# A two-block network in fp32 on one core: weight splits in pieces of 512 columns, broadcasts by transposes, and a reordered end of the last down projection

## The chip, the cores and the metric

The kernel runs on one core of one Trainium2 chip. The metric is the device time of one execution in microseconds (us); lower is better. Five engines of the core take part: TensorE (PE in the profile; its weight loads are listed apart as PEld), VectorE (DVE), ScalarE (ACT), GpSimd (POOL) and SyncE (SP), which issues the DMA transfers. Each engine works through its own list of instructions in order, and waits on semaphores for the others.

## The reference

256 tokens `x` and 256 context tokens `ctx` of width 1024 go through two networks of two layers each. What matters here, cut short:

```python
def first_block(x, c, ctx, c_ctx, ...):            # layer 0: convolution, layer 1: attention
    for i in range(DEPTH):
        hx = rmsnorm(x, norm_g[i, 0]) * (1.0 + sc_x) + sh_x
        ...                                          # conv_module or attention_module
        x = x + g_x * rmsnorm(yx, norm_g[i, 1])
        fx = rmsnorm(x, norm_g[i, 2]) * (1.0 + scf_x) + shf_x
        x = x + gf_x * rmsnorm(swiglu(fx, ffn_w1[i], ffn_w3[i], ffn_w2[i]), norm_g[i, 3])
    return x

def second_block(x, ...):
    for l in range(DEPTH):
        mix = token_mixing(x, ...)                   # three branches, two of them attention
        x = layer_norm(ALPHA * x + mix, ln1_g[l], ln1_b[l])
        ffn = conv_ffn(x, ...)                       # (gelu(a) * u) @ w_down
        x = layer_norm(ALPHA * x + ffn, ln2_g[l], ln2_b[l])
    return x
```

All matrices are fp32, and the result has to have about fp32 accuracy.

## The kernel before

**Products.** Activations lie transposed, features on the 128 partitions and tokens along the free dimension. A product in fp32 accuracy is made of three products in the reduced type fp32r: both operands are split into a rounded part "hi" and the rest "lo", and `mm3` (or `mm_late`, the same in another order) adds hi·hi, hi·lo and lo·hi in PSUM. The tiles of hi and lo parts are called `round` in the profile (`late` where they share room that an earlier phase gave up); everything else in SBUF is `plain`, and PSUM tiles are `bank`.

**Weights.** All weights lie in one DRAM tensor `wts`, in chunks of 128 x 2048 in the order of use. `Stream.next` issues a chunk's DMA, and `Stream.split` makes hi and lo of each half of it (128 x 1024): ScalarE copies the half to hi (a CAST with rounding), VectorE subtracts hi from the source to get lo. Three chunks may be in flight and five halves of hi and lo may be held.

**Normalisations.** `rms` and `ln_stats` sum over features on TensorE, get one number for each token, `y`, with the tokens on partitions, raise it to the power -0.5 on GpSimd (`rsqrt`), and call `spread`, which turns `y` into a PSUM tile that has the token's number in every partition: for each block of 128 tokens a plain fp32 matmul of the broadcast column `y[:, t:t+1]` with the identity matrix. `rms` spreads 2 blocks; `ln_stats` spreads mean and scale, 4 blocks each at the convolution's end and 2 blocks each elsewhere; `diff_norm` in `mixing` spreads twice 4 blocks in each of its two layers. `normed` in `layer1` does the same with its own code for the keys, twice 4 blocks. Counted over the program these are 62 matmuls of `spread` (26 from `rms`, 20 from `ln_stats`, 16 from `diff_norm`) and 8 of `normed`, 70 in all. `trans` in `layer1` and in `mixing` transposes 128 x 128 blocks of attention weights by TensorE's transpose, with the same identity.

**The last down projection.** `conv_ffn` of the last layer calls `updown` with `tokens`: here the product with `w_down` is made with tokens on the partitions, in four PSUM banks, one for each block of 128 tokens (t = 0, 1) and half of the 1024 outputs (o = 0, 1). `down_tokens(c)` adds the two hidden tiles of chunk c; the last chunk is c = 10. Then `final` normalises and writes block t = 0 and then t = 1: two BN_STATS, BN_AGGR, an addition, the power on GpSimd and a small product, then for each half an activation on ScalarE, a product and an addition on VectorE, and the DMA of 128 x 512 to `out`.

**What sets the order.** Nothing runs when the code above is called: `Recorder` notes every instruction and what it depends on, and `schedule` puts all of them in an order by a list scheduler with costs for each instruction (`cost`: 111 ns for a transpose, about 220 ns for a plain fp32 matmul of 128 columns; for VectorE and ScalarE a constant and a slope), in several rounds, of which it keeps the best. `emit` then issues them in that order from one line (L889 of the profile, so lines tell nothing apart), and `fills` puts idle-time fillers, plain 128 x 128 matmuls of identity by identity into an unused bank, into those gaps of the plan in which TensorE would stand still (L883). So a change of a single operation can move any instruction of the program.

Of the kernel before, what the change touches and what calls it, by code (L numbers as in the profile page):

```python
# [10 lines left out]
F32 = mybir.dt.float32  # L11
# [8 lines left out]
D = 1024  # L20
T = 256
KT = 8
FT = 22
# [16 lines left out]
FOLD1 = 2  # L40
ROUNDS = 6
SWITCH = 95
RUSH = 20e3
FILL = 0.7

# [859 lines left out]
class Stream:  # L905
# [18 lines left out]
    def split(self, src):  # L924
        n = src.shape[1]
        hi, lo = (self.pool.tile([128, HALF], F32R, tag=g, bufs=self.nsp) for g in ("hi", "lo"))
        self.nc.scalar.copy(hi[:, :n], src)
        self.nc.vector.tensor_sub(lo[:, :n], src, hi[:, :n].bitcast(F32))
        return hi, lo


class Kern:
# [145 lines left out]

    def spread(self, out, y):

        n = y.shape[-1]
        for t in range(n):
            self.nc.tensor.matmul(out[:, t * 128:t * 128 + 128], y[:, t:t + 1].to_broadcast([128, 128]), self.cst("ident"),
                                  start=(t == 0), stop=(t == n - 1))

    def feature_means(self, tiles, tag):

# [471 lines left out]
    def layer1(self):  # L1559
        nc, tc, xs = self.nc, self.tc, self.xs  # L1560
        with ExitStack() as es:
# [19 lines left out]
            def normed(src, g, name):  # L1581

                y = head_rms(src)
                b, ye = self.bank("tp", "hr"), self.s512("ye")
                nc.scalar.copy(ye.rearrange("p (a b) -> p a b", a=8), y[:, :, None].to_broadcast([128, 8, 64]))
                for t in range(4):
                    nc.tensor.matmul(b[:, t * 128:t * 128 + 128], ye[:, t * 128:t * 128 + 128], self.cst("ident"),
                                     start=(t == 0), stop=(t == 3))
                q = self.s512(name)
                nc.scalar.mul(q, src, g)  # L1590
                nc.vector.tensor_mul(q, q, b)
                return q
# [150 lines left out]
    def updown(self, up_, label, banks, tokens=None):  # L1743

        hs = {}

        def down_tokens(c):
            w = self.ws.next(label + (c,))
            last = c == FT // 2 - 1
            if last:  # L1750
                order = [(kk, t, o) for t in range(2) for o in range(2) for kk in range(2)]
            else:
                order = [(kk, t, o) for kk in range(2) for t in range(2) for o in range(2)]
            for kk, t, o in order:
                k, cols = 2 * c + kk, slice(t * 128, t * 128 + 128)
                self.mm3(banks[2 * t + o], hs[k][0][:, cols], hs[k][1][:, cols], *w.hl(kk * D + o * 512, 512),
                         k == 0, k == FT - 1)
            if c == 0:
                tokens()

        def down(c):
            if tokens:
                return down_tokens(c)
            w = self.ws.next(label + (c,))
            last = c == FT // 2 - 1
            if last:
                order = [(kk, m) for m in range(8) for kk in range(2)]
            else:
                order = [(kk, m) for kk in range(2) for m in range(8)]
            for kk, m in order:  # L1770
                k, b = 2 * c + kk, kk * 8 + m
                self.mm3(banks[m // 2][:, (m % 2) * T:(m % 2) * T + T], *w.hl(b * 128, 128), hs[k][0], hs[k][1],
                         k == 0 and m % 2 == 0, k == FT - 1 and m % 2 == 1)

        for j in range(FT):
            hs[j] = up_(j)
            if j >= 2 and j % 2 == 0:
                down(j // 2 - 1)
        down(FT // 2 - 1)
# [559 lines left out]
```

## Time and profile before

| what | value |
|---|---|
| time before, median of 3 runs | 1916.68 us (1913.9 to 1918.26) |
| the profiled execution's own time | 1914.48 us |
| its span from the first to the last instruction | 1912.7 us |
| mean granted TensorE clock | 0.997 |
| TensorE busy | 1885.2 us, 99% of the span |
| VectorE busy | 1398.7 us, 73% |
| ScalarE busy | 1094.4 us, 57% |

The profile is of one execution. Its own time is 1.8 us longer than its span, and 2.2 us below the median of the runs. Busy time counts an engine from an instruction's start to its end, waits excluded. A plain fp32 matmul shows as two records in the trace, an fp32r matmul and a transpose as one.

### The profile page before, as it was taken

To read this page: it belongs to the slowest core of one execution; us is meant where nothing else is said; L and a number is where in the kernel's file an instruction comes from. 1 tells how busy PE (TensorE), PEld (TensorE's weight loads), DVE (VectorE), ACT (ScalarE), POOL (GpSimd) and SP (SyncE) were. 2 spreads that over 40 slices of the span, in tenths; PEclk is the share of its full clock that TensorE was granted. 3 is DMA by queue.
4 is the path that set the end of the run, shared out by engine and by line. 5 is a ranking of instruction groups with operands and counts; after the bars stand their busy time and mean duration, and the time that the engine had idled before them with its cause. 6 is when DMAs were issued, how large, how long until landed. Compare 5 with 4: busy or idle time off the path is not lost.

```text
span 1912.7 us, 35502 instructions
## 1 busy us (share of the span) xinstructions
PE 1885.2 (99%) x14444; PEld 1721.3 (90%) x14444; DVE 1398.7 (73%) x2535; ACT 1094.4 (57%) x1913; POOL 321.9 (17%) x297
## 2 busy tenths in 40 slices
PE   8999999999999999999999999999999999999997
PEld 5765988999998878999999999999999999998997
DVE  5996878878877686655479755786679976577666
ACT  5576845444535587544557555575567665556554
POOL 0674000000001311000032001331114200123001
PEclk9999999999999999999999999999999999999999
DMA  8367534323325441455434544444544444454552
GB/s 351 132 231 304 186 125 162 122 98 111 114 93 192 154 155 67 175 179 198 155 135 155 179 155 154 156 177 176 199 139 174 150 182 155 155 166 166 190 185 88
DMA packets 44949, 312.53 MB, mean 163 GB/s; under 512 B 5489, under 2 KB 5745, under 8 KB 8433
## 3 DMA queue, kind: packets, MB, share of 16 engines
q1 hardware_dynamic: 44784, 310.26, 45.0%
q8 instruction: 113, 1.85, 0.4%
q14 instruction: 52, 0.42, 0.1%
HBM read 309.19 MB, written 1.05 MB: 162 GB/s over the span
## 4 chain that ended last, share of the span: by engine, by line
PE 87%; DVE 6%; ACT 4%; DMA 1%; issue 1%; POOL 0%; SPq 0%; DVEq 0%; POOLq 0%; ACTq 0%
PE bank L889 87%; DVE plain L889 3%; DVE round L889 3%; ACT plain L889 2%; ACT round L889 2%; PE bank L883 1%; DMA plain<-vecs 0%; POOL plain L889 0%; DVE late L889 0%; DMA plain<-wts 0%; DMA plain<-xin 0%; ACT L889 0%; ACT early L889 0%; SPq L889 0%; POOLq L2334 0%
## 5 line engine op out<-in xcount | busy, mean ns | idle before, releaser
L889 PE MATMUL bank<-round 128*128 128x256 f32 (+2 forms) x8912 | 1185.9, 291 | 2.9 <-ACT round L889 1.8
L889 PEld LDWEIGHTS bank<-round 128*128 128x128 f32 x8912 | 1120.6, 189 | 53.0 <-issue 17.5
L889 DVE TENSOR_TENSOR round<-plain,round 128x1024 fp32r<-128x1024 f32 (+2 forms) x581 | 659.0, 1153 | 314.5 <-ACT round L889 311.7
L889 ACT CAST round<-plain 128x1024 fp32r<-128x1024 f32 (+4 forms) x573 | 547.1, 974 | 437.2 <-PE bank L889 390.7
L889 PE MATMUL bank<-late,round 128*128 128x256 f32 (+1 forms) x2780 | 408.1, 300 | 1.3 <-DVE late L889 1.0
L889 PEld LDWEIGHTS bank<-late,round 128*128 128x128 f32 x2780 | 373.8, 191 | 24.3 <-issue 4.0
L889 POOL TENSOR_TENSOR plain<-plain 128x256 f32<-128x256 f32 (+6 forms) x181 | 212.2, 1183 | 848.0 <-DVE plain L889 538.1
L889 PE MATMUL bank<-plain 128*128 128x128 f32 (+9 forms) x1894 | 217.4, 373 | 11.2 <-ACT plain L889 9.3
L889 ACT ACTIVATE plain<-plain 128x256 f32<-128x256 f32 (+6 forms) x361 | 152.3, 446 | 106.1 <-DVE plain L889 90.1
L889 PEld LDWEIGHTS bank<-plain 128*32 128x32 f32 (+4 forms) x1894 | 132.5, 141 | 64.8 <-issue 27.1
L889 DVE TENSOR_TENSOR plain<-plain 128x256 f32<-128x256 f32 (+6 forms) x324 | 135.2, 445 | 23.8 <-ACT plain L889 10.5
L889 DVE TENSOR_TENSOR plain<-plain,bank 128x256 f32<-128x256 f32 (+1 forms) x236 | 115.2, 508 | 40.4 <-PE bank L889 32.6
L889 ACT COPY plain<-bank 128x512 f32<-128x512 f32 (+5 forms) x189 | 92.1, 503 | 75.9 <-PE bank L889 70.9
L889 POOL MEMSET late<- 64x1024 f32 (+2 forms) x14 | 8.6, 612 | 649.6 <-PE bank L889 649.2
L889 ACT ACTIVATE plain<-bank,plain 128x256 f32<-128x256 f32 (+3 forms) x171 | 95.9, 602 | 28.4 <-PE bank L889 12.3
L889 ACT CAST late<-plain 128x256 fp32r<-128x256 f32 (+2 forms) x114 | 56.2, 493 | 75.2 <-DVE plain L889 58.7
L889 POOL TENSOR_TENSOR plain<-plain,early 128x512 f32<-128x512 f32 x79 | 89.5, 1135 | 55.5 <-ACT early L889 51.4
L889 DVE SCALAR_TENSOR_TENSOR bank<-early,plain,bank 128x512 f32<-128x512 f32 x130 | 90.4, 749 | 1.0
L889 ACT ACTIVATE round<-plain 128x256 fp32r<-128x256 f32 (+2 forms) x128 | 62.8, 534 | 30.8 <-DVE plain L889 19.6
L889 DVE SCALAR_TENSOR_TENSOR plain<-plain,bank 128x256 f32<-128x256 f32 (+1 forms) x138 | 63.9, 508 | 19.4 <-PE bank L889 18.9
L889 DVE TENSOR_TENSOR late<-plain,late 128x256 fp32r<-128x256 f32 (+2 forms) x106 | 57.2, 540 | 17.4 <-ACT late L889 17.3
L889 PE MATMUL bank<-round,late 128*128 128x512 f32 x264 | 63.3, 393 | 1.4 <-ACT late L889 1.2
(61 smaller groups left out, 785.5 us busy)
## 6 DMA issues: line engine op xcount, KB each, us to landing
plain<-wts SPq DMA_DIRECT2D x280, 1024.0 KB, 4.8
plain<-wts SPq DMA_DIRECT2D x8, 768.0 KB, 4.2
plain<-xin SPq DMA_DIRECT2D x2, 1024.0 KB, 7.3
early<-wts SPq DMA_DIRECT2D x2, 1024.0 KB, 16.7
plain<-wts SPq DMA_DIRECT2D x2, 840.0 KB, 4.4
plain<-lnv SPq DMA_DIRECT2D x2, 512.0 KB, 4.6
out<-plain SPq DMA_DIRECT2D x4, 256.0 KB, 2.0
plain<-consts SPq DMA_DIRECT2D x1, 736.0 KB, 9.7
```

Of the source, the lines that this page charges most:

```text
L883: self.nc.tensor.matmul(self.banks[b][:, :128], *map(real, fill), start=True, stop=True)
L889: getattr(on, name)(*map(real, a), **{n: real(x) for n, x in k.items()})
```

## The change

Three edits, and a constant `PART = 512`:

```diff
@@ class Stream @@
     def split(self, src):
         n = src.shape[1]
         hi, lo = (self.pool.tile([128, HALF], F32R, tag=g, bufs=self.nsp) for g in ("hi", "lo"))
-        self.nc.scalar.copy(hi[:, :n], src)
-        self.nc.vector.tensor_sub(lo[:, :n], src, hi[:, :n].bitcast(F32))
+        for c in range(0, n, PART):
+            s = slice(c, min(c + PART, n))
+            self.nc.scalar.copy(hi[:, s], src[:, s])
+            self.nc.vector.tensor_sub(lo[:, s], src[:, s], hi[:, s].bitcast(F32))
         return hi, lo
@@ class Kern @@
     def spread(self, out, y):
-        n = y.shape[-1]
-        for t in range(n):
-            self.nc.tensor.matmul(out[:, t * 128:t * 128 + 128], y[:, t:t + 1].to_broadcast([128, 128]), self.cst("ident"),
-                                  start=(t == 0), stop=(t == n - 1))
+        for t in range(y.shape[-1]):
+            self.nc.tensor.transpose(out[:, t * 128:t * 128 + 128], y[:, t:t + 1].to_broadcast([128, 128]), self.cst("ident"))
@@ layer1, normed @@
                 for t in range(4):
-                    nc.tensor.matmul(b[:, t * 128:t * 128 + 128], ye[:, t * 128:t * 128 + 128], self.cst("ident"),
-                                     start=(t == 0), stop=(t == 3))
+                    nc.tensor.transpose(b[:, t * 128:t * 128 + 128], ye[:, t * 128:t * 128 + 128], self.cst("ident"))
@@ updown @@
         def down_tokens(c):
-            w = self.ws.next(label + (c,))
-            last = c == FT // 2 - 1
-            if last:
-                order = [(kk, t, o) for t in range(2) for o in range(2) for kk in range(2)]
+            ws[c] = self.ws.next(label + (c,))
+            end = FT // 2 - 2
+            if c < end:
+                order = [(2 * c + kk, t, o) for kk in range(2) for t in range(2) for o in range(2)]
+            elif c == end:
+                order = [(2 * c + kk, 0, o) for kk in range(2) for o in range(2)]
             else:
-                order = [(kk, t, o) for kk in range(2) for t in range(2) for o in range(2)]
-            for kk, t, o in order:
-                k, cols = 2 * c + kk, slice(t * 128, t * 128 + 128)
-                self.mm3(banks[2 * t + o], hs[k][0][:, cols], hs[k][1][:, cols], *w.hl(kk * D + o * 512, 512),
+                order = [(2 * c + kk, 0, o) for o in range(2) for kk in range(2)]
+                order += [(2 * end + kk, 1, o) for o in range(2) for kk in range(4)]
+            for k, t, o in order:
+                cols = slice(t * 128, t * 128 + 128)
+                self.mm3(banks[2 * t + o], hs[k][0][:, cols], hs[k][1][:, cols], *ws[k // 2].hl(k % 2 * D + o * 512, 512),
                          k == 0, k == FT - 1)
```

In counts: 487 splits of 1024 columns and 6 of 840 or 560 become two pieces each, so that VectorE and ScalarE issue 493 instructions more each; 70 plain matmuls become 70 transposes. All other counts stay, but for the fillers, 154 before and 129 after.

Since everything is scheduled anew, the order moves throughout. Three places follow, in which `round` tiles on VectorE are weight parts unless said otherwise.

VectorE at the end of layer 0's feed-forward part, from the last `rsqrt` of the first token group (TENSOR_SCALAR from a bank of 128x2) to the modulation that uses its spread (SCALAR_TENSOR_TENSOR with bank_68); the TENSOR_TENSOR of 128x2x256 are sums of the down projection. Before:

```order
L889 TENSOR_TENSOR round<-plain,round 128x1024 [waits DMAHW4_49,Activation_49]
L889 TENSOR_TENSOR plain<-plain,bank_65 128x2x256 [waits PE_49]
L889 TENSOR_SCALAR plain<-bank_70 128x2 [waits PE_49]
L889 TENSOR_TENSOR plain<-plain,bank_64 128x2x256 [waits PE_49]
L889 TENSOR_TENSOR round<-plain,round 128x1024 [waits Activation_49]
L889 SCALAR_TENSOR_TENSOR plain<-plain,bank_68 128x256 [waits PE_49]
```

And after the change:

```order
L890 TENSOR_TENSOR plain<-plain,bank_65 128x2x256 [waits PE_49]
L890 TENSOR_TENSOR round<-plain,round 128x512 [waits Activation_49]
L890 TENSOR_SCALAR plain<-bank_67 128x2 [waits PE_49]
L890 TENSOR_TENSOR round<-plain,round 128x512 [waits Activation_49]
L890 TENSOR_TENSOR round<-plain,round 128x512 [waits PE_49,Activation_49]
L890 TENSOR_TENSOR plain<-plain,bank_63 128x2x256 [waits PE_49]
L890 SCALAR_TENSOR_TENSOR plain<-plain,bank_68 128x256 [waits PE_49]
```

The whole split that stood between the last sum and the modulation is gone; two pieces stand between the `rsqrt` and the last sum.

VectorE at the end of layer 1's feed-forward part, around the `rsqrt` of its output (TENSOR_SCALAR from bank_70); DMAHW7 and DMAHW0 mark the first piece of two consecutive chunks of weights, `late` is the last hidden tile. Before:

```order
L889 TENSOR_TENSOR round<-plain,round 128x1024 [waits DMAHW7_49,PE_49,Activation_49]
L889 TENSOR_TENSOR late<-plain,late 128x256 [waits Activation_49]
L889 TENSOR_TENSOR round<-plain,round 128x1024 [waits PE_49,Activation_49]
L889 TENSOR_TENSOR round<-plain,round 128x1024 [waits DMAHW0_49,PE_49,Activation_49]
L889 TENSOR_SCALAR plain<-bank_70 128x2 [waits PE_49]
L889 TENSOR_TENSOR plain<-plain,bank_70 128x256 [waits PE_49]
```

And after the change:

```order
L890 TENSOR_TENSOR round<-plain,round 128x512 [waits DMAHW7_49,PE_49,Activation_49]
L890 TENSOR_TENSOR round<-plain,round 128x512 [waits PE_49,Activation_49] x3
L890 TENSOR_SCALAR plain<-bank_70 128x2 [waits PE_49]
L890 TENSOR_TENSOR round<-plain,round 128x512 [waits DMAHW0_49,Activation_49]
L890 TENSOR_TENSOR round<-plain,round 128x512 [waits Activation_49]
L890 TENSOR_TENSOR plain<-plain,bank_70 128x256 [waits PE_49]
```

Three halves of chunks stood ahead of the `rsqrt`, the third of them the next chunk's first. Now the two halves of the one chunk, in four pieces, stand ahead, and the next chunk's first half stands behind, where VectorE waits for the spread. On ScalarE one piece stands ahead of the COPY of the sums, one between it and the next chunk's pieces, where a whole CAST stood on each side of it. The end of layer 1's attention part has changed in the same way.

VectorE in `final`, at the program's end. Before, block t = 0 has bank_64 and bank_65, block t = 1 bank_66 and bank_63:

```order
L889 BN_STATS plain<-bank_63 128x6 [waits PE_49]
L889 BN_AGGR plain<-plain 128x2 [waits DVE_49]
L889 SCALAR_TENSOR_TENSOR plain<-plain 128x1 [waits Pool_49]
L889 TENSOR_SCALAR plain<-plain 128x1 [waits DVE_49]
L889 SCALAR_TENSOR_TENSOR plain<-plain 128x1 [waits Pool_49]
L889 TENSOR_TENSOR plain<-plain 128x512 [waits Activation_49] x2
L889 TENSOR_TENSOR plain<-plain 128x512 [waits DVE_49]
L889 TENSOR_TENSOR plain<-plain 128x512 [waits Activation_49]
L889 TENSOR_TENSOR plain<-plain 128x512 [waits DVE_49]
```

After the change t = 0 has bank_66 and bank_65, t = 1 bank_63 and bank_64:

```order
L890 SCALAR_TENSOR_TENSOR plain<-plain 128x1 [waits Pool_49]
L890 BN_STATS plain<-bank_64 128x6 [waits PE_49]
L890 BN_AGGR plain<-plain 128x2 [waits DVE_49]
L890 TENSOR_TENSOR plain<-plain 128x512 [waits Activation_49]
L890 TENSOR_SCALAR plain<-plain 128x1 [waits DVE_49]
L890 TENSOR_TENSOR plain<-plain 128x512 [waits Activation_49]
L890 TENSOR_TENSOR plain<-plain 128x512 [waits DVE_49]
L890 SCALAR_TENSOR_TENSOR plain<-plain 128x1 [waits Pool_49]
L890 TENSOR_TENSOR plain<-plain 128x512 [waits DVE_49]
L890 TENSOR_TENSOR plain<-plain 128x512 [waits Activation_49] x2
```

The last BN_STATS, of the bank that TensorE finishes last, stands behind the small product of block 0, which waits for GpSimd; and the small product of block 1 stands behind three of the four large products and additions of block 0. On TensorE 11 matmuls of 512 columns follow the last one of block 0, where 7 followed before.

## Rows read from the trace of the kernel before

**Rows 1.** The page, part 1: busy time and share of each engine.

```profile
PE 1885.2 (99%) x14444; PEld 1721.3 (90%) x14444; DVE 1398.7 (73%) x2535; ACT 1094.4 (57%) x1913; POOL 321.9 (17%) x297
```

**Rows 2.** Groups by form, PE: count, busy us, mean ns; idle before, its releasers.

```profile
L889 PE MATMUL bank<-round 128*128 128x256 f32 x7792 | 974.9, 283 | 2.0 <-ACT round L889 1.2 <-DVE round L889 0.5
...
L889 PE MATMUL bank<-plain 128*128 128x128 f32 x458 | 68.2, 276 | 2.0 <-POOL plain L889 1.7 <-ACT plain L889 0.2
...
L883 PE MATMUL bank<-plain 128*128 128x128 f32 x308 | 43.0, 282 | 0.0
```

**Rows 3.** Timeline, PE: start, us, records; a spread in layer 0, a `trans` in layer 1.

```profile
245.91 0.61 PE L889 MATMUL bank<-plain 128*128 128x128 f32 x4
...
691.00 0.60 PE L889 MATMUL bank<-plain 128*128 128x128 f32 x4
```

**Rows 4.** Groups by form, DVE and ACT, whole span: splits of 1024 and of 512.

```profile
L889 DVE TENSOR_TENSOR round<-plain,round 128x1024 fp32r<-128x1024 f32 x487 | 605.7, 1261 | 313.9 <-ACT round L889 311.5 <-PE bank L889 1.1
...
L889 DVE TENSOR_TENSOR round<-plain,round 128x512 fp32r<-128x512 f32 x33 | 22.4, 684 | 0.2
...
L889 ACT CAST round<-plain 128x1024 fp32r<-128x1024 f32 x487 | 503.7, 1051 | 397.6 <-PE bank L889 366.5 <-issue 17.3 <-DMA plain<-wts 8.9
...
L889 ACT CAST round<-plain 128x512 fp32r<-128x512 f32 x33 | 20.4, 621 | 24.7 <-PE bank L889 20.3 <-DVE plain L889 4.4
```

**Rows 5.** Timeline, DVE, ACT, PE: ends of layer 1's attention (752) and feed-forward.

```profile
752.42 2.45 DVE L889 TENSOR_TENSOR round<-plain,round 128x1024 fp32r<-128x1024 f32 x2 [6.08 <-ACT round L889]
...
953.93 1.18 ACT L889 CAST round<-plain 128x1024 fp32r<-128x1024 f32 x1
954.86 0.51 ACT L889 COPY plain<-bank 128x256 f32<-128x256 f32 x1
...
955.14 2.44 DVE L889 TENSOR_TENSOR round<-plain,round 128x1024 fp32r<-128x1024 f32 x2 [7.49 <-ACT round L889]
955.43 0.61 PE L889 MATMUL bank<-plain 128*128 128x1 f32 x4
...
957.50 0.15 DVE L889 TENSOR_SCALAR plain<-bank 128x2 f32<-128x2 f32 x1
```

**Rows 6.** Timeline, PE and DVE, 604 to 608 us: end of layer 0.

```profile
604.73 0.71 PE L889 MATMUL bank<-plain 128*128 128x128 f32 x4
...
605.38 1.22 DVE L889 TENSOR_TENSOR round<-plain,round 128x1024 fp32r<-128x1024 f32 x1
...
607.59 1.69 PE L889 MATMUL bank<-round 128*128 128x256 f32 x12 [0.59 <-ACT round L889]
```

**Rows 7.** Timeline, ACT, DVE and PE, 41 to 45 us: second chunk of `pw1`.

```profile
41.79 1.98 ACT L889 CAST round<-plain 128x1024 fp32r<-128x1024 f32 x2
...
42.85 2.36 DVE L889 TENSOR_TENSOR round<-plain,round 128x1024 fp32r<-128x1024 f32 x2 [0.52 <-ACT round L889]
...
44.13 4.22 PE L889 MATMUL bank<-round 128*128 128x512 f32 x17
```

**Rows 8.** Windows 990:1051.5, 1247:1273.5, 1465:1517.2, 1713:1738.2: their sum.

```profile
sum 165.40, PE 159.53 PEld 152.87 DVE 156.69 ACT 132.62 POOL 59.08; mean PE 39.88 PEld 38.22 DVE 39.17 ACT 33.15 POOL 14.77
```

**Rows 9.** Groups by form, DVE splits of 1024, first and last of these windows.

```profile
L889 DVE TENSOR_TENSOR round<-plain,round 128x1024 fp32r<-128x1024 f32 x15 | 20.6, 1387 | 0.1
...
L889 DVE TENSOR_TENSOR round<-plain,round 128x1024 fp32r<-128x1024 f32 x7 | 8.8, 1260 | 0.0
```

**Rows 10.** Timeline, all engines, 1893 to 1910 us: the program's end.

```profile
1893.04 9.74 PE L889 MATMUL bank<-round,late 128*128 128x512 f32 x42
...
1902.82 0.70 DVE L889 BATCH_NORM_STATS2 plain<-bank 128x6 f32<-128x512 f32 x1
...
1903.82 2.78 ACT L889 ACTIVATE plain<-bank,plain 128x512 f32<-128x512 f32 x4 [6.25 <-DVE plain L889]
1904.03 0.56 POOL L889 TENSOR_TENSOR plain<-plain 128x1 f32<-128x1 f32 x1 [0.50 <-DVE plain L889]
...
1904.70 4.91 DVE L889 TENSOR_TENSOR plain<-plain 128x512 f32<-128x512 f32 x8
```

More of the change, by code (lines that the diff above doesn't have):

```diff
@@ L42 @@
 SWITCH = 95
+PART = 512
 RUSH = 20e3
@@ L1745, in updown @@
         hs = {}
+        ws = {}
         def down_tokens(c):
-            w = self.ws.next(label + (c,))
-            last = c == FT // 2 - 1
-            if last:
-                order = [(kk, t, o) for t in range(2) for o in range(2) for kk in range(2)]
-            else:
-                order = [(kk, t, o) for kk in range(2) for t in range(2) for o in range(2)]
-            for kk, t, o in order:
-                k, cols = 2 * c + kk, slice(t * 128, t * 128 + 128)
-                self.mm3(banks[2 * t + o], hs[k][0][:, cols], hs[k][1][:, cols], *w.hl(kk * D + o * 512, 512),
+            ws[c] = self.ws.next(label + (c,))
[4 more added lines that the diff above has]
+                order = [(2 * c + kk, 0, o) for kk in range(2) for o in range(2)]
+            else:
+                order = [(2 * c + kk, 0, o) for o in range(2) for kk in range(2)]
[3 more added lines that the diff above has]
+                self.mm3(banks[2 * t + o], hs[k][0][:, cols], hs[k][1][:, cols], *ws[k // 2].hl(k % 2 * D + o * 512, 512),
                          k == 0, k == FT - 1)
```

## The prediction

> **What bounds the kernel now.** First the busy times: TensorE works 1885.2 of 1912.7 us, VectorE 73%, ScalarE 57% [rows 1]. So nearly all of the time is TensorE's own work, and 27.5 us are its idle time. Then the groups of TensorE by form: the 7792 products of 256 columns have 2.0 us of idle time ahead of them in all, that is, weights and activations are almost always there in time; but 308 records are fillers, 43.0 us of them [rows 2], and these stand where the plan had nothing to do. Idle time and fillers make 70.5 us in which nothing is computed, the start and the end of the program included. The change can gain in three ways: fewer TensorE records, less of those 70 us, or a shorter end. It can lose in one: more instructions on VectorE and ScalarE, where these are full.
>
> **Transposes for matmuls.** A spread of two blocks stands as four records of 0.61 us; four transposes of `trans` stand as four records of 0.60 us too [rows 3]. Two matmuls and four transposes thus take the same time: a plain matmul of 128 columns is two records. With 0.276 us for one record alone [rows 2] the distance from one to the next is (0.61 - 0.276) / 3 = 0.111 us, and (0.60 - 0.276) / 3 = 0.108 us for a transpose. The 70 exchanged matmuls are 140 records, 15.5 us; 70 transposes are 7.6 us. That saves **8.0 us**. It counts where TensorE is busy throughout, and as much where it waits, since the spread is itself a link of the chain from sums to scaled activations. The trace has no transpose of a broadcast column; the bounds are one record as in `trans` (-8.0) and two as now (0). I take the first: operand shapes and the identity are the same as in `trans`. [...]
>
> **Splits in two pieces: what they cost.** 493 splits become 986 pieces. On VectorE two splits back to back take 2.36 us [rows 7] and one 1.22 [rows 6], so they follow each other at 1.14 us; eight 512-column operations take 4.91 us [rows 10], one of them 0.684 [rows 4], so these follow each other at 0.604 us. A split in two pieces costs VectorE 2 x 0.604 - 1.14 = 0.07 us more, by full durations at most 2 x 0.684 - 1.261 = 0.107 [rows 4]. On ScalarE the bound by durations is 2 x 0.621 - 1.051 = 0.19 us [rows 4]. Over the whole program that is 35 us more on VectorE; it stands idle for 514 us [rows 1], and the splits wait 314 us in front of them, nearly all of it for ScalarE, which in turn waits for TensorE to give buffers back (366.5 us) [rows 4]. The cover is thus TensorE's work on weights that are held already; without it the price would be the full 35 us. There are stretches without cover: in four windows of together 165.4 us, two in the mixing phases and two around layer norms, VectorE is busy 156.7 us, 95%, while TensorE too stands only 5.9 us [rows 8]. In them lie 15 splits in the first, 7 in the last [rows 9], 45 in all with the 10 and 13 of the two between. All of it on the path would be 45 x 0.07 = 3.1 us; none of it 0, and a half of a chunk that is there 0.6 us sooner could even give a little back. I take **+1.5**, the middle, since TensorE there is neither free nor waiting much.
>
> **Splits in two pieces: what they give.** Where a short and urgent operation stands behind a long split, a shorter piece lets it through.
> - End of layer 1: the COPY of the sums at 954.86 stands behind a CAST that started at 953.93, and the `rsqrt`, whose sums TensorE has at 955.43 + 0.61 = 956.04, starts only at 957.50, when two splits end [rows 5]. With one piece ahead the COPY comes some 0.46 us sooner (half a CAST's distance, 1.98 - 1.05 = 0.93 [rows 7]); the last subtraction ahead of the `rsqrt` is then that of the piece behind the COPY, which ends near 956.2. The `rsqrt` moves from 957.5 to about 956.2: **-1.3**, and TensorE does nothing but fillers until the chain is through.
> - End of its attention: the same two splits, 752.42 to 754.87, ahead of the `rsqrt` [rows 5]. -1.3 again, but the order has a new gap with fillers ahead of the last products there; I take **-0.8**.
> - End of layer 0: the spread is done at 604.73 + 0.71 = 605.44, but a split from 605.38 to 606.60 keeps VectorE from the modulation, and TensorE's product starts at 607.59 [rows 6]. In the new order no split stands there, and a sum that is done earlier: **-1.0**.
> - Start: the CASTs of the second `pw1` chunk begin at 41.79, VectorE can begin at 42.85, and TensorE's steady work at 44.13 [rows 7]. Half a CAST (0.46) and half a subtraction (0.57) sooner would be 1.0; I take **-0.7**, since the table load beside it and the next chunk may take some back.
>
> **The end of the program.** TensorE ends at 1893.04 + 9.74 = 1902.78, and the last VectorE operation at 1904.70 + 4.91 = 1909.61, 6.83 later [rows 10]. The diff gives block 0 a longer lead: 11 matmuls of 0.23 us instead of 7 follow it. If block 0 were through by then, its four operations of 0.61 us would leave the end, less what VectorE waits. But the order does not allow it. Block 0's banks are full 2.5 us before TensorE ends; three BN_STATS of 0.70, the aggregation, the addition and the power of 0.56 follow, so its small product comes near +0.4 us from TensorE's end. Only behind it stands the last BN_STATS, to +1.1; then aggregation and three of block 0's large operations, to about +3.4, and only then block 1's small product. With 0.69 for ScalarE (2.78 / 4) and four more operations of 0.61 the end is near +6.65 [rows 10]. I take **-0.2**, with the bounds 0 and -1.7.
>
> **The sum.** -8.0 + 1.5 - 1.3 - 0.8 - 1.0 - 0.7 - 0.2 = -10.5 us. The profiled execution took 1914.5 us, its span and 1.8 around it; that gives 1904.0 for it. The median of the runs shown is 2.2 above that execution, so the median after is forecast at **1906 us**, 0.55% less. About 0.2% (3.8 us) is what a measurement of this kernel can tell from no change.
>
> **The rivals.**
> - *More of the waiting goes.* Fillers fall from 154 to 129, and most of those missing stood in the four full windows; if the stalls there (5.9 us idle and the fillers between) fall by half instead of growing, and the end gains its bound, the sum is -8.0 - 3.8 - 3 - 1.7 = -16.5: 1900. For it: splits of 1.26 to 1.39 us in those windows [rows 9] are the longest operations of a full engine. Against it: VectorE has more to do there, not less.
> - *Only the transposes count.* The boundaries give nothing, since some other operation stands in front, and the full windows cost their 3.1: -8.0 + 3.1 = -4.9, 1912.
> - *A transpose of a broadcast column is no shorter, or its time is not on the path.* Then -3.8 + 1.5 - 0.2 = -2.5, 1914, no change. Against it: rows 3.
> - *Slower: the fixed cost of each instruction decides in the full windows.* If there each split costs its upper bound on VectorE and ScalarE in series, 0.107 + 0.19 = 0.30 us, the 45 cost 13.4 us; with nothing from the boundaries, -8.0 - 0.2 + 13.4 = +5.2, 1922. It decides from 0.18 us for a split in these windows. For it: splits there take 1.39 us in the first window instead of 1.26 in the mean [rows 4, 9], so VectorE is held up by something. Against it: the engines work on different pieces at once, and ScalarE is free a fifth of the time there [rows 8]. [...]
>
> **Chances.** Forecast (-7 to -14) 0.52; more waiting goes 0.18; only transposes 0.16; no shorter 0.08; slower 0.06. The first two and most of the third lie beyond 3.8 us: faster 0.82, same 0.12, slower 0.06. The range leaves out the last two and the ends: 1898 to 1913; the forecast's own is 1902.5 to 1909.5.
>
> **What the profile after would show.** Transposes: the group of plain 128x128 records outside the fillers falls from 458 to 388, a spread of two blocks is two records. Pieces: near 980 splits of 512 at about 0.68 us on VectorE, whose busy time rises by 35 to 55 us; if the windows of rows 8 grow by more than 3 us, the cost is mis-sized. Boundaries: the `rsqrt` near 957 follows its sums within 0.3 us; no split between spread and modulation near 605. End: the last operation 6.5 to 6.8 us behind TensorE's last product; 5 would prove my reading of the order wrong. The prediction is wrong as a whole if TensorE's busy time outside fillers does not fall by about 8 us, or if new idle time shows in the middle of a phase, since the whole order is made anew.

## The result: 1% faster, nearly twice the forecast

| | before | after |
|---|---|---|
| median | 1915.48 us (1913.9 to 1918.26, 4 runs) | 1896.32 us (1895.65 to 1897.67, 4 runs) |
| ratio | | 0.9900 [0.9888, 0.9911] |
| span of the profiled execution | 1912.7 us | 1894.8 us |
| TensorE idle in the span | 27.5 us | 25.6 us |

The time fell by 19.2 us, where 10.5 were forecast; 1896.3 lies 1.7 us below the range. Part 1 of the page after, beside [rows 1]:

```profile
PE 1869.2 (99%) x14324; PEld 1706.6 (90%) x14324; DVE 1463.6 (77%) x3028; ACT 1145.3 (60%) x2406; POOL 311.4 (16%) x297
```

VectorE works 65 us more (forecast 35 to 55), ScalarE 51 us more, and the program is shorter all the same: TensorE has 16.0 us less to do. Its groups by form, beside [rows 2]:

```profile
L890 PE MATMUL bank<-round 128*128 128x256 f32 x7792 | 973.2, 283 | 2.1 <-ACT round L890 1.6 <-DVE round L890 0.2 <-DVE plain L890 0.2
...
L890 PE MATMUL bank<-plain 128*128 128x128 f32 x388 | 59.7, 276 | 2.7 <-ACT plain L890 1.6 <-POOL plain L890 0.9
...
L884 PE MATMUL bank<-plain 128*128 128x128 f32 x258 | 35.8, 282 | 0.0
```

The plain records fell from 458 to 388 as forecast (70 transposes with one record each for 70 matmuls with two), the fillers from 308 to 258. Idle time and fillers together fell from the 70.5 us of before to 25.6 + 35.8 = 61.4, by 9.1 us. The splits, beside [rows 4]:

```profile
L890 DVE TENSOR_TENSOR round<-plain,round 128x512 fp32r<-128x512 f32 x1013 | 709.4, 736 | 236.9 <-ACT round L890 228.2 <-PE bank L890 0.9
...
L890 ACT CAST round<-plain 128x512 fp32r<-128x512 f32 x1013 | 587.3, 622 | 363.2 <-PE bank L890 326.5 <-DMA plain<-wts 12.3 <-issue 6.2
```

A subtraction of 512 columns takes VectorE 736 ns in the mean, 52 more than the 684 of before on which the forecast's upper bound rested.

Two of the boundaries, on the timeline. The end of layer 1, beside [rows 5]:

```profile
947.50 0.75 ACT L890 CAST round<-plain 128x512 fp32r<-128x512 f32 x1
...
948.01 0.51 ACT L890 COPY plain<-bank 128x256 f32<-128x256 f32 x1
...
948.58 0.61 PE L890 MATMUL bank<-plain 128*128 128x1 f32 x4
...
949.69 0.15 DVE L890 TENSOR_SCALAR plain<-bank 128x2 f32<-128x2 f32 x1
...
953.10 2.17 PE L890 MATMUL bank<-round 128*128 128x256 f32 x16 [0.28 <-ACT round L890]
```

The COPY stands behind one CAST of 512 columns, and the `rsqrt` starts 0.50 us behind its sums (948.58 + 0.61 = 949.19); before it was 957.50 - 956.04 = 1.46, and the forecast had 0.3. The end of layer 0, beside [rows 6]:

```profile
603.28 0.41 PE L890 MATMUL bank<-plain 128*128 128x128 f32 x2
...
603.76 2.43 DVE L890 SCALAR_TENSOR_TENSOR plain<-plain,bank 128x256 f32<-128x256 f32 x6
...
604.83 1.45 PE L890 MATMUL bank<-round 128*128 128x256 f32 x10
```

From the spread's start to the first product it is 1.55 us, before 607.59 - 604.73 = 2.86. And the program's end, beside [rows 10]:

```profile
1876.66 8.63 PE L890 MATMUL bank<-round,late 128*128 128x512 f32 x37
...
1885.25 0.16 DVE L890 SCALAR_TENSOR_TENSOR plain<-plain 128x1 f32<-128x1 f32 x1 [0.67 <-POOL plain L890]
1885.33 0.70 DVE L890 BATCH_NORM_STATS2 plain<-bank 128x6 f32<-128x512 f32 x1
...
1888.14 0.15 DVE L890 SCALAR_TENSOR_TENSOR plain<-plain 128x1 f32<-128x1 f32 x1
...
1889.14 2.57 DVE L890 TENSOR_TENSOR plain<-plain 128x512 f32<-128x512 f32 x4 [0.24 <-ACT plain L890]
```

TensorE ends at 1885.29, VectorE at 1891.71, 6.42 later; before 6.83, forecast 6.5 to 6.8. Block 0's small product, the last BN_STATS and block 1's small product stand in the order that the forecast read.

**Where the time came from.** If the n-th fp32r product is sought in both traces, the same work can be compared stretch by stretch, with bounds where TensorE waits for nothing and no other work has moved across. The two profiled executions lie 17.9 us apart. The first 280 us became 1.8 us shorter; 570 to 783 us, with the ends of layer 0 and of the attention, 3.7; 902 to 965 us, the end of layer 1, 2.3. Four stretches that hold the four windows in which VectorE is full [rows 8] are next; this is the sum of the view by windows for before (965 to 1110, 1190 to 1330, 1445 to 1602 and 1700 to 1880 us), the first number being their length:

```profile
sum 622.00, PE 616.00 PEld 589.47 DVE 485.04 ACT 388.54 POOL 133.09; mean PE 154.00 PEld 147.37 DVE 121.26 ACT 97.14 POOL 33.27
```

and for the same work after (957.3 to 1098.8, 1178.6 to 1318.1, 1432.4 to 1586.6 and 1684.5 to 1862.5 us):

```profile
sum 613.20, PE 609.00 PEld 583.72 DVE 512.25 ACT 408.37 POOL 125.16; mean PE 152.25 PEld 145.93 DVE 128.06 ACT 102.09 POOL 31.29
```

They gave 8.8 us, although VectorE works 27 us more there; the stretches between them gave about 1 and the end 0.4. The largest single part thus came from the place where the forecast saw a loss.

### The profile page after: what moved, and what is told of

The parts are those of the page before. It is cut to its first block, busy times and chain, and to the rows that moved or that the text cites. A ratio compares the mean times of both kernels' runs of the same rounds, so it can differ in the third digit from the quotient of the medians.

```text
span 1894.8 us, 36440 instructions
## 1 busy us (share of the span) xinstructions
PE 1869.2 (99%) x14324; PEld 1706.6 (90%) x14324; DVE 1463.6 (77%) x3028; ACT 1145.3 (60%) x2406; POOL 311.4 (16%) x297
## 4 chain that ended last, share of the span: by engine, by line
PE 85%; DVE 7%; ACT 4%; issue 1%; DMA 1%; POOL 1%; SPq 0%; DVEq 0%; POOLq 0%; ACTq 0%
PE bank L890 84%; DVE plain L890 4%; DVE round L890 3%; ACT plain L890 2%; ACT round L890 2%; POOL plain L890 1%; PE bank L884 1%; DMA plain<-wts 1%; DVE late L890 0%; DMA plain<-vecs 0%; ACT late L890 0%; ACT L890 0%; DMA plain<-xin 0%; ACT early L890 0%; SPq L890 0%
## 5 line engine op out<-in xcount | busy, mean ns | idle before, releaser
L890 DVE TENSOR_TENSOR round<-plain,round 128x512 fp32r<-128x512 f32 (+2 forms) x1074 | 732.3, 719 | 236.9 <-ACT round L890 228.2
L890 ACT CAST round<-plain 128x512 fp32r<-128x512 f32 (+2 forms) x1066 | 607.8, 613 | 374.9 <-PE bank L890 327.2
L890 POOL TENSOR_TENSOR plain<-plain 128x256 f32<-128x256 f32 (+6 forms) x181 | 206.5, 1150 | 848.5 <-DVE plain L890 514.7
L890 PE MATMUL bank<-plain 128*32 128x256 f32 (+8 forms) x1824 | 208.9, 377 | 10.4 <-ACT plain L890 9.0
L890 PEld LDWEIGHTS bank<-plain 128*32 128x32 f32 (+4 forms) x1824 | 123.2, 137 | 63.2 <-issue 27.6
L890 DVE SCALAR_TENSOR_TENSOR plain<-bank,plain 128x255 f32<-128x255 f32 (+2 forms) x152 | 62.4, 467 | 9.9 <-ACT plain L890 9.4
```

The lines of the kernel that those rows point to most:

```text
L890: getattr(on, name)(*map(real, a), **{n: real(x) for n, x in k.items()})
```

## The experiments

Theories after the result: the transposes count in full or not; the pieces gain by what the planner can do with them (short operations in between, halves that are ready sooner), or by the cost that the planner takes for them, or the order is a lucky one. Each run was compared with the kernel before on the same chip; differences between two runs are given below as those of their medians. The ratios follow these within about 2 us: the change's own ratio rests on 4 runs of the kernel before, whose median is 0.7 to 1.5 us above that of the later sets. The last column lists the stretches ahead of the program's end in which the profile shows a granted TensorE clock of 0.50, half of full speed. Each 3.4 us of them are counted below as 1.7, their half, as an estimate; the last section measures 1.4 to 1.5. The column is of the one profiled execution: in u1 and c1 that was 2.9 and 2.6 us slower than the median, so it need not hold for the median there.

| run | median us | ratio to before | at 0.50, us |
|---|---|---|---|
| before | 1914 to 1915 | 1 | 3.4 |
| the change | 1896.32 | 0.9900 [0.9888, 0.9911] | 3.4 |
| e1 transposes alone | 1912.36 | 0.9981 [0.9971, 0.9990] | 6.8 |
| e2 pieces alone | 1906.06 | 0.9952 [0.9937, 0.9967] | 3.4 |
| e3 down order alone | 1915.03 | 0.9997 [0.9988, 1.0006] | none |
| e4 change, pieces joined | 1905.20 | 0.9944 [0.9927, 0.9961] | 6.8 |
| f1 before's order, transposes | 1910.56 | 0.9981 [0.9971, 0.9990] | 3.4 |
| f2 before's order, pieces | 1923.85 | 1.0044 [1.0027, 1.0061] | 3.4 + 3.4 |
| p1 before, new order | 1913.95 | 0.9993 [0.9984, 1.0003] | 3.4 |
| g1 transposes and pieces | 1896.24 | 0.9903 [0.9888, 0.9917] | none |
| c1 transposes, longer cost | 1901.01 | 0.9931 [0.9916, 0.9946] | 3.4 |
| u1 change, matmuls wait for both pieces | 1904.81 | 0.9953 [0.9938, 0.9967] | 6.8 + 3.4 |
| r1 change's order, matmuls | 1905.18 | 0.9951 [0.9936, 0.9966] | 3.4 |
| h1 pieces of 256 | 1915.92 | 1.0013 [1.0002, 1.0025] | none |
| q1 change, new order | 1897.88 | 0.9915 [0.9900, 0.9930] | 3.4 |
| c2 longer cost alone | 1905.99 | 0.9962 [0.9947, 0.9977] | 3.4 + 3.4 |
| c3 c1, new order | 1901.38 | 0.9936 [0.9919, 0.9953] | none |
| a1 change, cost 10% longer | 1905.53 | 0.9955 [0.9940, 0.9970] | 6.8 + 3.4 |
| k1 change, pieces adjacent | 1908.36 | 0.9965 [0.9953, 0.9976] | 6.8 + 3.4 |
| a3 change, cost of before | 1903.47 | 0.9949 [0.9935, 0.9964] | 3.4 + 3.4 |

**One part at a time (e1, e2, e3).** Each takes one of the three edits of the diff into the kernel before.

> The kernel before with the 70 transposes alone. If they are worth their records, and other stalls stay as they are, -8 to -9 us: 1906 to 1908. If much of the 19 us comes from the new order that any edit brings, it lies outside 1903 to 1911. In the trace the plain 128x128 records outside the fillers fall from 458 to 388 in either case.

> The kernel before with splits in pieces of 512 alone. Theory P (a piece lets short urgent operations through, in the full windows too): -8 to -11 us, 1905 to 1908, with idle time and fillers falling by as much. The prediction's own sum for the pieces is -2.3 (boundaries -3.8, full windows +1.5): 1913. Rival by cost alone: +3, 1918.

> The kernel before with the reordered end of the last down projection alone. The order in which VectorE gets its work at the end decides: -0.2 to -0.5 us, 1915, and the last VectorE operation ends about 6.4 to 6.8 us behind TensorE's last product. If the lead of block 0 can be used when the plan is made for this edit alone, -1.7: 1913.8. An effect on the rest of the program through a new order would show as more than that.

By the ratios transposes gave 3.6 us, pieces 9.2, the down product's order nothing that can be measured. In sum that is 12.8, not 19.2.

**Both pieces as one operation of the plan (e4).** The planner sees one operation with the cost of two pieces; the pieces are issued one behind the other (cut short, as are the diffs below; comments are added).

```diff
-        for c in range(0, n, PART):
-            self.nc.scalar.copy(hi[:, s], src[:, s])
-            self.nc.vector.tensor_sub(lo[:, s], src[:, s], hi[:, s].bitcast(F32))
+        o = rec.record(lane, name, args(parts[0]), {})    # for ScalarE, then for VectorE
+        for s in parts[1:]:
+            rec.join(o, lane, name, args(s), {})
```

> The changed kernel, but the two pieces of a split are planned as one operation, so that nothing is put between them; semaphores still pass piece by piece. Theory P (what counts is that other operations get in between): most of the pieces' gain goes, +7 to +11 us over the changed kernel, 1903 to 1907. Rival E (what counts is that the first piece is there earlier for TensorE): it stays, 1896 to 1899.

8.9 us of the gain were gone.

**The order of before kept (f1, f2).** The planner sees the old instruction; only when it is issued does it become transposes (f1) or two pieces (f2).

```diff
+                    if k.pop("flip", False):            # f1: set on the 70 matmuls
+                        on.transpose(*a)
+                        continue
+                    part = k.pop("part", 0)             # f2: set on a split's copy and subtraction
+                    if part:
+                        for c in range(0, n, part):
+                            getattr(on, name)(*[x[:, c:min(c + part, n)] for x in a])
+                        continue
                     getattr(on, name)(*a, **k)
```

> The kernel before, planned with its 70 matmuls of 128 columns, and so with its order unchanged on every engine; only when the instructions are written out do the 70 become transposes. Theory A (a transpose saves 0.11 us each on the path, and the new order that the planner makes took 4.4 us of the 8.0 back in the run with transposes alone): the time falls by 8.0 us, +-1.5, to about 1907, and the spreads stand as two records in place of four. Theory B (the saving lies beside other work, so that it never was 8 us): the time falls by 3.6 us or less, to 1911 to 1915.

> The kernel before, planned with splits of up to 1024 columns, and so with its order unchanged; each split is written out as pieces of 512 that follow each other on their engine with nothing between. Theory O (the gain of the pieces comes from what the planner puts between them and how early it starts them): no gain, from 0 to +5 us, since only the 0.07 us for each split on VectorE is left. Theory L (the gain comes from a first half that is ready 0.5 us sooner, whatever the order): a good part of the 9.2 us that the pieces alone gave, -4 us or more.

f1 has the ratio of e1, so no loss by e1's new order is seen. Part 1 of its page:

```profile
PE 1878.3 (98%) x14374; PEld 1713.5 (90%) x14374; DVE 1399.2 (73%) x2535; ACT 1094.5 (57%) x1913; POOL 323.2 (17%) x297
```

and a spread of two blocks on its timeline:

```profile
245.62 0.38 PE L891 MATMUL bank<-plain 128*128 128x128 f32 x2
```

TensorE's work fell by 6.9 us and the span (1908.9) by 3.8: its idle time grew from 27.5 to 30.6. The transposes are as short as forecast, but in the order of before nearly half of what they save turns into waiting for others. f2 came out worse than either theory had it, 9 us slower. The same work in the four stretches (969.0 to 1114.7, 1194.6 to 1336.0, 1451.0 to 1610.3 and 1708.2 to 1889.0 us):

```profile
sum 627.20, PE 616.85 PEld 589.82 DVE 509.21 ACT 408.58 POOL 121.01; mean PE 154.21 PEld 147.45 DVE 127.30 ACT 102.15 POOL 30.25
```

That is 5.2 us more than before, 4.35 of it TensorE's idle time (627.20 - 616.85 = 10.35 in place of 6.0), and nearly all lies in the windows of [rows 8] themselves, 170.5 us in place of 165.4. The first 280 us take 4.3 more (1.7 of it for the second stretch at 0.50).

**A new order for the same work (p1, q1).** `SWITCH = 96` in place of 95 in the kernel before (p1) and in the change (q1); it changes the order on every engine, but only a little.

> The kernel before with one number of its planner changed, the cost of a change of tiling from 95 to 96 ns; the work is the same, the order is made anew in nearly every place. Theory R (any new order moves the time by several us, and the part of the gain that the forecast lacks may be luck): the time moves by 3 us or more, up or down. Theory S (orders for the same work differ little, so the gain is the pieces'): it stays within 1.5 us.

> The change with the planner's cost of a change of tiling at 96 in place of 95 ns; the same work, the order made anew. The same step moved the kernel before by -0.8 us. Theory S (the gain belongs to the pieces and the transposes): 1894 to 1899. Theory R (the order of the change is a lucky one among many): 1901 or more.

Both stayed within 1.6 us. That is a weak test for luck: if the instructions of two traces are lined up by operation, tiles and shape, VectorE and ScalarE keep 97 to 99% of their order in p1 and q1. In the runs below that change only what the planner assumes for a piece, VectorE keeps 62% (a3), 78% (a1), 84% (k1) and 87% (u1), and all of them execute the change's instructions 7 to 12 us slower. Whether the change's order is a lucky one among many is thus not settled.

**Without the down product's order (g1).** The diff without its third part.

> The change without the new order of the last down product: transposes and pieces together. The parts alone gave -3.6, -9.2 and 0, in sum -12.8, all three together -19.2. Theory T (transposes and pieces support each other, the down product's order is worth nothing): as the whole change, 1895 to 1898. Theory D (the order of the down products is worth something once the rest is done): 1901 or more.

1896.24: transposes and pieces together are the whole change.

**The change's order with the old matmuls (r1).** The planner sees transposes, issued are matmuls, as in f1 the other way round.

> The change with its order as planned on every engine, but the 70 transposes written out as the matmuls of before. Theory T (with splits in pieces TensorE is the bound nearly throughout, so that the transposes count in full, while in the order before about half of it turned into waiting): 7 to 9 us above the change, 1903 to 1906. Theory U (the transposes are worth 4 us in any order): 3 to 5 us above it, 1899 to 1901.

8.9 us slower; the transposes count in full here. TensorE's busy time is 8.1 us above the change's 1869.2, by part 1 of r1's page:

```profile
PE 1877.3 (99%) x14394; PEld 1714.8 (90%) x14394; DVE 1463.8 (77%) x3028; ACT 1145.7 (60%) x2406; POOL 312.4 (16%) x297
```

What is left without them, in the four stretches (sum of the view by windows, r1, 962.2 to 1103.8, 1183.7 to 1323.4, 1438.0 to 1594.3 and 1692.2 to 1870.5 us):

```profile
sum 615.90, PE 610.81 PEld 586.07 DVE 512.11 ACT 408.28 POOL 125.88; mean PE 152.70 PEld 146.52 DVE 128.03 ACT 102.07 POOL 31.47
```

Pieces and their order gave 622.0 - 615.9 = 6.1 us in these stretches. Their fillers alone, before and in r1 (the same view for the fillers' line):

```profile
sum 622.00, PE 8.08 PEld 7.37; mean PE 2.02 PEld 1.84
...
sum 615.90, PE 4.98 PEld 4.52; mean PE 1.24 PEld 1.13
```

So 3.1 of the 6.1 us are fillers that are not needed any more, and 0.9 idle time (6.0 to 5.1); the rest is TensorE's other records, which take less time in the new order, and no view here says why.

**Only the planner's cost of a split (c2, c1, c3).** As e4, but written out as one instruction: VectorE and ScalarE execute exactly the splits of before, and the planner holds each for 68 ns longer on VectorE and 93 on ScalarE. c2 is that alone, c1 with the transposes, c3 is c1 with `SWITCH = 96`.

```diff
+            o.calls = [(lane.real, name, args(slice(0, n)), {})]
```

> Transposes, and a planner that takes each split for as long as its two pieces together, while the split is written out as one instruction; TensorE's order is that of the run with joined pieces (1905.2). Theory H (pieces help on the chip even where they follow each other directly, since the first half is ready sooner): as the transposes alone, 1909 to 1913. Theory C (it was the planner's longer cost of a split that made a better order): 1905 or less.

> The kernel before, its planner taking each split for as long as two pieces (68 ns more on VectorE and 93 on ScalarE for 1024 columns), written out as one instruction; no transposes, the work of before. Theory C (the planner's cost of a split was too short, and a longer one gives a better order by itself): 1903 to 1910. Theory R (the run with transposes and the longer cost met a lucky order): 1912 to 1916.

> Transposes and the longer planned split (1901.0), with the cost of a change of tiling at 96 in place of 95 ns. Theory C (the longer cost makes the better order, whatever its details): 1899 to 1904. Theory R (that order was lucky): 1907 to 1913, as the transposes alone.

Here lay the surprise: c2 is 8 us faster than before with the same instructions in another order. Its four stretches (963.6 to 1105.6, 1185.5 to 1327.1, 1441.8 to 1597.9 and 1695.8 to 1870.6 us):

```profile
sum 614.50, PE 611.06 PEld 587.22 DVE 482.85 ACT 389.06 POOL 134.09; mean PE 152.77 PEld 146.81 DVE 120.71 ACT 97.27 POOL 33.52
```

7.5 us shorter than before, with TensorE's idle time there at 614.5 - 611.06 = 3.4 us in place of 6.0. The end of layer 1 became shorter too, with whole splits, here c2 beside [rows 5]:

```profile
954.30 0.61 PE L890 MATMUL bank<-plain 128*128 128x1 f32 x4
...
955.15 0.15 DVE L890 TENSOR_SCALAR plain<-bank 128x2 f32<-128x2 f32 x1
```

and f2, pieces in the order of before:

```profile
959.82 0.61 PE L899 MATMUL bank<-plain 128*128 128x1 f32 x4
...
961.53 0.15 DVE L899 TENSOR_SCALAR plain<-bank 128x2 f32<-128x2 f32 x1
```

The `rsqrt` starts 0.24 us behind its sums in c2 and 1.10 in f2; before it was 1.46, in the change 0.50. At this place the order does more than the pieces.

c3 repeats c1 with a nearly equal order (VectorE and ScalarE keep more than 99% of it). And c1 and e4 have the same order on TensorE: writing a split as two adjacent pieces costs 4.2 us there, perhaps 1.7 of them for a longer stretch at 0.50.

**The cost of a piece (a3, a1).** The change, its planner taking two pieces for as long as the one instruction of before (a3: factors 0.9435 on VectorE and 0.9105 on ScalarE), or for 10% longer (a1: 1.1 on both, as one factor `self.slow`). The edit of a3:

```diff
-        o.dur += self.cost(lane.eng, name, a, k, o)
+        o.dur += self.cost(lane.eng, name, a, k, o) * self.scale.get(lane.eng, 1.0)
```

> The change, but its planner takes the two pieces of a split together for only as long as the one instruction of before (a piece of 512 columns 34 ns shorter on VectorE and 46 on ScalarE than in the change). Theory C (part of the change's gain is that the planner holds splits for longer, as in the run with the longer cost alone, -8): 1902 to 1908. Theory E (with halves that can be used at once the cost doesn't matter): 1894 to 1899.

> The change, its planner taking each piece of a split for 10% longer (60 ns on VectorE, 52 on ScalarE); the same work. Theory C (a planner that holds splits for longer than they are when they follow each other makes better orders, since in full stretches they take longer): 1890 to 1895. Theory N (602 and 522 ns are the right cost, and the order only changes): 1895 to 1900.

Both ways 7 to 9 us are lost (1.7 and 3.4 of them to more time at 0.50). In a1 both theories fell: longer isn't better without end, and a new order for the same work isn't as good by itself.

**Short operations in between, or halves used sooner (u1, k1).** In u1 the planner lets a matmul depend on all of a hi or lo tile; in k1 a second piece follows right behind the first on its engine, ahead of everything else.

```diff
+            if lane.eng == "PE" and t.wait:             # u1, hi and lo tiles
+                m = (1 << 2 * t.size) - 1
```

```diff
+            if c:                                       # k1, x: the first piece
+                for o, x in zip(pair, first):
+                    o.preds[x.i], o.mate, o.rush = x, x, 1e9
```

> The change, but its planner lets every matmul wait for both pieces of a split; the pieces are still planned and issued one by one on ScalarE and VectorE. Theory P (the gain over joined pieces comes from short operations that get in between two pieces): nearly all of it stays, 1896 to 1899. Theory E (it comes from matmuls that the planner starts on the first half): it is lost, 1903 or more.

> The change with the second piece of a split bound to the first: on ScalarE and on VectorE it comes right behind it, so that nothing gets in between, while the planner still lets matmuls start on the first half. With the change (both), the run in which matmuls wait for both pieces (pieces free, no early half: 1904.8) and the run with joined pieces (neither: 1905.2) this makes a table of two by two. Theory E (the early half brings the gain over joined pieces): 1895 to 1899. Theory P (what gets in between brings it, and the other run met a bad order): 1903 to 1906.

With both freedoms 1896.3, with the first alone 1904.8, with the second alone 1908.4, with neither 1905.2. Even if 3.4 us are taken off u1 and k1, and 1.7 off e4, for their longer stretches at 0.50, one freedom alone gives 2 us at most of the 7. In these runs only both together do, and neither theory held. Each of the four is a single order, though, so a good or bad order is not excluded here either.

**Shorter pieces (h1).** `PART = 256`.

> The change with pieces of 256 columns in place of 512. By the distances of instructions that follow each other, 1.141 us for 1024 columns and 0.602 for 512, an instruction's fixed part is about 0.063 us, so a split costs VectorE 0.13 us more again, some 60 us in all. Theory P (short operations get through sooner still): as the change or up to 4 us better, 1892 to 1897. Theory F (the fixed part decides in the stretches where VectorE is full, 45 splits): 6 us or more above it, 1902 to 1910.

All of the gain was lost. In the four stretches (968.2 to 1111.4, 1191.3 to 1331.5, 1445.7 to 1603.8 and 1701.7 to 1880.6 us):

```profile
sum 620.40, PE 613.96 PEld 587.40 DVE 532.17 ACT 444.33 POOL 127.32; mean PE 153.49 PEld 146.85 DVE 133.04 ACT 111.08 POOL 31.83
```

That is 7.2 us more than in the change, about what theory F had for the full windows (45 x 0.13 = 5.9), though in another order. But the larger part, 14 of the 20 us, is lost in the first 280, where neither theory looked. Two rows of h1's timeline:

```profile
127.29 15.89 DVE L890 SCALAR_TENSOR_TENSOR bank<-early,plain,bank 128x512 f32<-128x512 f32 x24
...
132.77 8.87 PE L884 MATMUL bank<-plain 128*128 128x128 f32 x78
```

VectorE works without a pause from 100 to 143 us (view by windows, h1: busy 43.00 of 43.00 us; the change 38.06). In the last 15.9 us of it there are 24 steps of the convolution's taps with no split between, and meanwhile TensorE gets 78 records of fillers.

## Why the prediction was wrong

**Transposes: right in size, not in where they count.** Forecast -8.0; -8.9 in the change (r1), 6.9 us of TensorE's time in f1. That the saving counts "as much where it waits" failed for the order of before: there it was worth 3.6 us by the ratio (e1, f1). Two blocks in 0.38 us (f1) in place of 0.61 [rows 3], and 8.1 us of TensorE's time for 70 transposes in r1, 0.116 each, show one record in place of two.

**Splits in full windows: the step that failed.** The forecast was +1.5, bounds 0 to +3.1: a price of 0.07 us for each of 45 splits, in an order taken as given. Measured without the transposes it is -6.1 in the stretches around these windows (r1). The price itself is real, and larger than the bound: with the order held, pieces cost 5.2 us there (f2), 0.12 us for each of the 45. f2 doesn't tell fixed cost from waiting in an order that was planned for something else. What the step left out is that the list scheduler makes the whole order anew from its costs. Shown is: the longer planned cost alone gives 8 us with no instruction changed (c2); with the old cost the change loses 7 (a3); with the longer cost the pieces, planned freely, are worth 4.7 us on top (c1 to the change), and in the runs made that took both freedoms (u1, k1, e4).

**Boundaries: near in size, not by the pieces alone.** Without the transposes (r1 against before, same work): end of layer 1 -2.0 (forecast -1.3); ends of layer 0 and of the attention together -1.5 (forecast -1.8); start -0.6 (forecast -0.7): the steady work on the second chunk of `pw1` began at 42.83 us in the change in place of 44.13 [rows 7], and from 44 to 100 us the n-th product comes 0.6 us sooner in both. That a shorter piece lets the `rsqrt` through is the smaller part of the gain at the end of layer 1: pieces in the old order took its wait from 1.46 to 1.10 us (f2), a new order without pieces to 0.24 (c2). So the size came out partly by luck. Not in the forecast at all: +1.3 in the rest of the first 280 us, and -0.9 between the four stretches.

**End: right.** -0.4 from TensorE's end (forecast -0.2), and nothing in e3 and g1.

So the sum's -10.5 lacked 7.6 us in the full windows (+1.5 forecast, -6.1 measured); all other terms and gaps together came to 1.1. The rival "more of the waiting goes" (1900) was nearest; its cause, that stalls in the full windows fall, was right in kind: idle time and fillers in the four stretches went from 14.1 to 10.1 us (r1). Its gain at the program's end did not come, and of the 50 filler records that went only 22 stood in the four windows, not most.

**Left open.** It is open why the longer cost makes the better plan. Splits of 1024 columns took 1387 ns in the first full window in place of 1261 in the mean [rows 4, 9], so a plan that counts them longer is nearer to the truth there; but a1, which goes further, loses. That is argued, not shown. The rival stays that the orders scatter by several us whatever the cost, and that those of the change and of c2 are good ones among them; p1, q1 and c3 keep too much of the order to exclude it. The parts don't add up either: transposes gave 3.6 us on the order of before, 5.0 from c2 to c1 (up to 1.7 of it perhaps by the clock), and 9 on the change's.

## What to carry to other kernels

Where a planner sets the order, an edit acts twice: by what its instructions cost on the chip, and by what the planner believes they cost. Hold the old order and exchange only the instructions, then change only the believed cost: two runs that tell these apart (here +9 and -8 us). A test for a lucky order has to change much of the order, so count how much of it a nudge leaves in place. And a saving on the busiest engine need not count in full: here the transposes gave 8.9 us in the new order, but 3.6 in the old, where TensorE's idle time grew from 27.5 to 30.6 us (f1). So look for what is late next, stretch by stretch.

## What was not expected of the hardware

In 16 of the 20 profiles the granted clock of TensorE falls to 0.50 in the middle of the program, for 3.4 or 6.8 us at a time. Two stretches of e1 (view by windows: length, TensorE's busy time and records, and so on; the clock is the third number from the end):

```profile
672.00:675.40 3.40, 3.40 (x19) 2.74 (x21) 1.40 (x5) 2.51 (x6) 2.97 (x2) 0.50 0.74 308
675.40:678.80 3.40, 3.40 (x17) 0.44 (x9) 2.26 (x7) 0.74 (x2) 1.88 (x1) 0.50 0.15 19
```

Ahead of it, at 666.72 to 671.9 us, TensorE had 24 records of plain products on tiles of 128*32, 15 records of products with two columns, and one wait of 0.33 us; that these are the cause is not shown. In the kernel before the stretch is 649.2 to 652.6 us, and on its timeline:

```profile
648.67 4.37 PE L889 MATMUL bank<-round 128*128 128x256 f32 x22
```

At the pace of the 12 products in [rows 6], (1.69 - 0.283) / 11 = 0.128 us, 22 take 2.97; so the stretch costs about 1.4 us, near the half of 3.4. e3 has TensorE's order of before but for the last 90 records, and no such stretch; the work from 570 to 783 us is 1.5 us shorter there. So the same order can run with the stretch or without. Before and the change have one such stretch each, so their difference doesn't hang on it; between the experiments, with none to 10.2 us of it, it makes up to about 4.5 us.
